# Sixteen modulation vectors of a two-layer fp32 mixer, summed on VectorE instead of multiplied on TensorE

## Chip, cores and metric

One core of a Trainium2 chip runs the whole program. The metric is the device time of one execution in microseconds (us); smaller is better. Engines are named as the profile names them: PE is TensorE's matmul, PEld its weight load, DVE is VectorE, ACT is ScalarE, POOL is GpSimd, SP is SyncE, which issues nearly all DMAs here.

## What is computed

Two layers over 512 latent tokens and 256 context tokens, width 1024, in fp32. Each layer makes shift, scale and gate vectors from two conditioning vectors (`c` and `c_ctx`), normalises the tokens with them, projects to twelve 512-wide sections and four 1024-wide gates, mixes the sections in four branches, and merges and projects them:

```python
mod_lat = jnp.dot(jax.nn.silu(c), w_mod) + b_mod          # [1024] x [1024, 3072]
mod_ctx = jnp.dot(jax.nn.silu(c_ctx), w_mod) + b_mod
sh_l, sc_l, g_l = jnp.split(mod_lat[:, None, :], 3, axis=-1)
z_lat = split_proj(jnp.dot(layer_norm(x) * (1.0 + sc_l) + sh_l, w_in) + b_in)
...                                                       # four branches: y_f, y_d, y_p, y_n
g = sigmoid(z[12].reshape(b, n, N_BRANCH, D_MODEL))
proj = einsum('bnie,ied->bnid', gated, w_branch)
out = einsum('bnd,de->bne', sum(g * proj, axis=2), w_out)
x_new = layer_norm(alpha * x + g_l * out_lat, ln_g, ln_b)
```

`w_mod` is 1024 x 3072 for each layer. The second layer takes no context output, so of its gate part only the latent vector is needed.

## The kernel before

Every fp32 product runs as three fp32r products of a high and a low part (`mm3`). Weights come in half tiles of 4 x 128 rows by 256 columns (512 KB) through one stream, `Stream`: `load` issues the DMA into a ring of three (`w_raw`), ACT casts the high part (`w_hi`, L333), DVE or POOL subtracts the low part (`w_lo`, L336), into rings of four. Jobs `take` their half tiles in the order of the list made by `jobs`; `ahead` splits the next ones during a job.

An order written out by hand sets everything else: `clk` counts modelled PE time, `chain` queues the steps behind a job with a delay each, and `turn_over`, called at each `yield` of a job, emits the steps that are due. Side work (attention, `side_na` and others) is a generator paced by the same clock. Each engine then runs its instructions in that order.

The stages of a layer: the first eight modulation columns (256 wide) of layer 0 ahead of everything; then the projections (`tok`, `rope`, `nat`), with the attention of the branches interleaved; the merges (`job_merge`, twelve jobs of a branch and a 256-wide column, each `gates`, `products`, `gates`, `products`), then `mgate` and `mproj` for the fourth branch; then `out`.

A modulation column is `job_mod`: it takes two half tiles, runs 16 matmuls with the conditioning vectors (4 columns: two vectors, high and low) as weights and 256 columns moving, ACT copies the 4 x 256 result (`rows`, L477), two small fp32 matmuls with `sel` turn it into columns (`turn`, L482), and DVE adds the bias (`add`, L488) into `modT`. Columns 8 to 11 of each layer stand between the halves of the `nat` sections 1, 5, 7 and 11, at the end of the projections; columns 0 to 7 of layer 1 stand behind the merges of branches 1 and 2 of layer 0.

PSUM tiles named `mm` are a ring of four banks (`mmt`). A merge part of layer 0 takes two of them (512 and 256 tokens), of layer 1 one.

Of the kernel before, what the change touches and what calls it, by code (L numbers as in the profile page):

```python
# [37 lines left out]
M_LAG = (0.4, 1.6, 2.0)  # L38
# [71 lines left out]
def emit(tc, A, out):  # L110
# [4 lines left out]
    def jobs():  # L115
        J = [("start",)] + [("mod", 0, c) for c in range(8)]
        for l in range(DEPTH):
# [59 lines left out]
    with ExitStack() as ctx, tc.manual_schedule():  # L177
# [4 lines left out]
        wr = pool("wr", 3)  # L182
        wp = pool("wp", 4)
# [169 lines left out]

        early = []
# [19 lines left out]
        cT = cp.tile([128, 8, 4], F32R, name="cT")  # L374

# [77 lines left out]
        def cond(ct):  # L453
            sg = vs.tile([16, 128], F32, name="csg", tag="vt")
            S.activation(sg, ct, AF.Sigmoid)
            V.tensor_tensor(out=ct, in0=ct, in1=sg, op=ALU.mult)
            ps = mmt()
            PE.transpose(ps[:, 0:16], ct, ident[:16, :16])
            pv = ps[:, 0:16].rearrange("p (v k) -> p k v", v=2)
            V.tensor_copy(cT[:, :, 0:2], pv)  # L460
            sub_lo(cT[:, :, 2:4], pv, cT[:, :, 0:2])

        def job_mod(l, c):
            hs = ws.take(2)
            ps = mmt()
            early_ = l == 0 and c < 8
            for k in range(8):
                for j in range(2):
                    mm(ps[0:4, 0:256], cT[:, k, :], hs[k // 4][j][:, k % 4, :], k == 0 and j == 0, k == 7 and j == 1)
                if k == (0 if early_ else 5):  # L470
# [20 lines left out]

            c2 = chain((M_LAG[0], rows), (M_LAG[1] if early_ else M_LAG[2], turn), (0.4, add), hold=[ps], reads=1, cls="mod", depth=1)

# [1231 lines left out]
        for j in J:  # L1725
# [39 lines left out]
            elif kind == "mod":  # L1765
# [5 lines left out]
                if l == 0 and j[2] < 8:  # L1771
                    for i in range(2, 6):
                        if X_AT[i - 2] == j[2]:
                            load_x(i)
                    norm_x(*X_NORM[j[2]])
# [23 lines left out]
            elif kind == "flag":  # L1799
                risen.append((j[1], [c for c in klass.get("tok", []) + klass.get("mt", []) if not c.done()]))  # L1800
# [29 lines left out]
            elif kind == "m_split":  # L1830
                finish_all()
                close_pool()
# [42 lines left out]
```

## Time and profile before

| | us |
|---|---|
| median of 3 runs (2042.03 to 2047.87) | 2044.71 |
| the profiled execution's own time | 2051.7 |
| its span | 2049.7 |
| PE busy | 1939.6 (95%) |
| DVE busy | 1145.4 (56%) |
| ACT busy | 899.5 (44%) |
| mean granted clock of TensorE, of full speed | 0.972 |

Busy time of PE is made of matmuls whose ends overlap, so the time that a group of matmuls takes is read from the starts of its first and of the next instruction in the timeline. The profiled execution is 2.0 us longer than its span, and 7.0 us over the median of the runs.

### The profile page before, as it was taken

What the parts mean: (1) busy time and instruction counts of PE and PEld (TensorE: products, weight loads), DVE (VectorE), ACT (ScalarE), POOL (GpSimd) and SP (SyncE); (2) the same over time, 40 slices, a digit from 0 to 9 for tenths busy, and PEclk for the clock granted to TensorE, in tenths of its full rate; (3) what the DMA queues carried; (4) which work ended last, traced back from release to release, by engine and by line L of the source; (5) the groups of instructions that cost most, each with busy time, mean ns of one, the idle gap of its engine ahead of it and who ended that gap; (6) DMA issues with size and microseconds to landing.
All of it is one profiled execution on the core that took longest, in us unless ns stands there. A gap on an engine that the chain in (4) does not pass through costs nothing.

```text
span 2049.7 us, 31044 instructions
## 1 busy us (share of the span) xinstructions
PE 1939.6 (95%) x11911; PEld 1679.0 (82%) x11911; DVE 1145.4 (56%) x2208; ACT 899.5 (44%) x1753; POOL 327.6 (16%) x322
## 2 busy tenths in 40 slices
PE   6999999988999999999999979998998999999996
PEld 3998888876888888888888979887877887888886
DVE  7636676554666432445316685577655775355368
ACT  5423465555566422323222254345554665333232
POOL 6321221201110000000000353122122210000013
PEclk9999999998999999999999979999999999999999
DMA  8423834335562531525212446364327655344344
GB/s 273 155 79 106 276 115 149 134 103 162 163 188 91 184 114 54 164 93 165 93 62 70 140 133 207 98 241 132 127 101 236 204 171 186 113 134 134 96 133 153
DMA packets 257396, 293.74 MB, mean 143 GB/s; under 512 B 25844, under 2 KB 220384, under 8 KB 256736
## 3 DMA queue, kind: packets, MB, share of 16 engines
q1 hardware_dynamic: 256672, 286.46, 43.6%
q0 software_dynamic: 576, 5.29, 0.7%
q8 instruction: 94, 1.54, 0.3%
q14 instruction: 54, 0.44, 0.1%
HBM read 230.82 MB, written 62.35 MB: 143 GB/s over the span
## 4 chain that ended last, share of the span: by engine, by line
PE 52%; DVE 7%; ACT 3%; DMA 2%; issue 2%; POOL 1%; SPq 0%; POOLq 0%; ACTq 0%; DVEq 0%
PE mm L268 46%; PE sd L268 4%; PE sd L272 1%; DMA w_raw<-in_w_out 1%; DVE w_lo L336 1%; DVE yt L1578 1%; DVE px0l L280 1%; DVE dp L955 1%; DMA w_raw<-in_w_in 0%; ACT w_hi L333 0%; ACT px0l L1046 0%; DVE dp L972 0%; PE mm L482 0%; DMA mtmp<-g 0%; DVE pws L797 0%
## 5 line engine op out<-in xcount | busy, mean ns | idle before, releaser
L336 POOL TENSOR_TENSOR w_lo<-w_raw,w_hi 128x512 fp32r<-128x512 f32 x148 | 208.3, 1418 | 1211.6 <-ACT w_hi L333 1136.8
L333 ACT CAST w_hi<-w_raw 128x512 fp32r<-128x512 f32 x520 | 300.0, 619 | 218.8 <-PE mm L268 113.9
L336 DVE TENSOR_TENSOR w_lo<-w_raw,w_hi 128x512 fp32r<-128x512 f32 x372 | 260.4, 732 | 202.9 <-ACT w_hi L333 201.4
L268 PE MATMUL mm<-px0h,w_hi 128*128 128x512 f32 x1216 | 339.2, 352 | 8.8 <-ACT w_hi L333 5.3
L268 PE MATMUL mm<-px0h,w_lo 128*128 128x512 f32 x1216 | 336.7, 350 | 0.6 <-DVE w_lo L336 0.6
L268 PE MATMUL mm<-px0l,w_hi 128*128 128x512 f32 x1216 | 334.1, 347 | 0.2 <-DVE px0l L1431 0.2
L268 PE MATMUL mm<-px1h,w_hi 128*128 128x512 f32 x864 | 290.8, 373 | 2.9 <-ACT sg L1471 2.3
L268 PE MATMUL mm<-px1h,w_lo 128*128 128x512 f32 x864 | 289.4, 371 | 0.0
L268 PE MATMUL mm<-px1l,w_hi 128*128 128x512 f32 x864 | 288.3, 370 | 0.0
L268 PEld LDWEIGHTS mm<-px0h,w_hi 128*128 128x128 f32 x1216 | 193.1, 191 | 39.8 <-ACT w_hi L333 6.3
L268 PEld LDWEIGHTS mm<-px0l,w_hi 128*128 128x128 f32 x1216 | 193.4, 191 | 31.3 <-issue 1.0
L268 PEld LDWEIGHTS mm<-px0h,w_lo 128*128 128x128 f32 x1216 | 192.3, 191 | 32.4 <-DVE w_lo L336 1.3
L268 PEld LDWEIGHTS mm<-px1h,w_hi 128*128 128x128 f32 x864 | 150.2, 189 | 32.0 <-ACT sg L1471 2.8
L268 PEld LDWEIGHTS mm<-px1h,w_lo 128*128 128x128 f32 x864 | 149.6, 189 | 28.3 <-issue 1.3
L268 PEld LDWEIGHTS mm<-px1l,w_hi 128*128 128x128 f32 x864 | 150.1, 189 | 27.6 <-issue 0.5
L268 PE MATMUL mm<-w_hi,px0h 128*128 128x256 f32 x480 | 144.5, 301 | 4.7 <-DVE px0h L552 4.3
L268 PE MATMUL mm<-w_lo,px0h 128*128 128x256 f32 x480 | 139.9, 292 | 6.7 <-POOL w_lo L336 6.0
L268 PE MATMUL mm<-w_hi,px0l 128*128 128x256 f32 x480 | 139.7, 291 | 0.7 <-DVE px0l L280 0.7
L268 PE MATMUL mm<-w_lo,px1h 128*128 128x256 f32 x384 | 112.4, 293 | 8.1 <-DVE w_lo L336 4.2
L268 PE MATMUL mm<-w_hi,px1h 128*128 128x256 f32 x384 | 114.3, 298 | 1.1 <-ACT w_hi L333 0.7
L268 PE MATMUL mm<-w_hi,px1l 128*128 128x256 f32 x384 | 111.5, 290 | 0.2 <-DVE px1l L280 0.2
L1503 DVE TENSOR_TENSOR mtmp<-mm,sg 128x512 f32<-128x512 f32 (+1 forms) x48 | 27.4, 599 | 142.9 <-PE mm L268 141.9
(234 smaller groups left out, 3110.3 us busy)
## 6 DMA issues: line engine op xcount, KB each, us to landing
w_raw<-in_w_in SPq DMA_DIRECT2D x160, 512.0 KB, 4.0
w_raw<-in_w_mod SPq DMA_DIRECT2D x36, 512.0 KB, 3.7
w_raw<-in_w_branch SPq DMA_DIRECT2D x32, 512.0 KB, 3.4
w_raw<-in_w_out SPq DMA_DIRECT2D x32, 512.0 KB, 3.5
w<-in_w_mod SPq DMA_DIRECT2D x12, 512.0 KB, 6.0
g<-ab SPq DMA_DIRECT2D x16, 384.0 KB, 2.7
nb<-bt SPq DMA_DIRECT2D x48, 128.0 KB, 4.7
y<-y SPq DMA_DIRECT2D x14, 384.0 KB, 4.9
```

The costliest lines, as they stand in the source:

```text
L268: PE.matmul(o, a, b, start=start, stop=stop)
L272: PE.transpose(o, i, idn)
L280: V.tensor_tensor(out=out_lo, in0=src, in1=hi.bitcast(F32), op=ALU.subtract)
L333: S.copy(x[1], x[0])
L336: e.tensor_tensor(out=x[2], in0=x[0], in1=x[1].bitcast(F32), op=ALU.subtract)
L955: V.tensor_scalar(out=p, in0=src, scalar1=-0.125, scalar2=None, op0=ALU.mult, op1=ALU.min, accum_out=mn)
L1503: V.tensor_tensor(out=o_[:, o:o + m], in0=ps[j][:, :m], in1=sg[:, o:o + m], op=ALU.mult)
L1578: V.scalar_tensor_tensor(out=y, in0=xs, scalar=ALPHA, in1=y, op0=ALU.mult, op1=ALU.add)
```

## The change

Sixteen of the 24 modulation columns leave `job_mod`: columns 8 to 11 of both layers and 0 to 7 of layer 1. They become jobs `vec`. Their weights no longer pass through `Stream`: they come by SP into a ring of two (`w_vec`) in fp32 and are not split. DVE multiplies each 128 x 256 slice by the conditioning vector's entry for its partition (`cS`, a copy of the conditioning vectors made at the start) and adds it up in `macc`: 8 steps for each vector and column, two vectors, or one where only the latent one is needed. The steps are spaced in modelled time (4 at 1.5, then 4 at 1.2). Then `total` sums over partitions with fp32 matmuls (`macc` as weights of 128 x 128, two columns of ones moving), and `add` puts the bias on. The twelve columns of layer 0's turn start behind the merges from the third of branch 0 to the last of branch 2, and behind the first two `mgate` jobs; the four of layer 1 behind its merges from the third of branch 0 on.

```diff
             for i, s in enumerate((1, 5, 7, 11)):
-                J += [("nat", l, s, 0), ("mod", l, 8 + i), ("nat", l, s, 1)]
-            mods = [("mod", l + 1, c) for c in range(8)] if l + 1 < DEPTH else []
+                J += [("nat", l, s, 0), ("nat", l, s, 1)]
+            mods = [("vec", l, 8 + i) for i in range(4)]
+            mods += [("vec", l + 1, c) for c in range(8)] if l + 1 < DEPTH else []
...
                         J += [("merge", l, b, s)]
-                        if b and mods:
+                        if mods and (b or s > 1):
                             J += [mods.pop(0)]
                 else:
-                    J += [("mgate", l, b, s) for s in range(4)] + [("mproj", l, b, s) for s in range(4)]
+                    for s in range(4):
+                        J += [("mgate", l, b, s)]
+                        if mods:
+                            J += [mods.pop(0)]
+                    J += [("mproj", l, b, s) for s in range(4)]
...
+        wm = pool("wm", 2)
...
+        class Vectors:
...
+            def load(self):
+                while self.nd < len(self.todo) and (self.nd < 2 or self.nd - 2 in self.ch and self.ch[self.nd - 2].done()):
+                    l, c, k = self.todo[self.nd]
+                    r = wm.tile([128, 4, 256], F32, name="w_vec", tag="w_vec")
+                    nc.sync.dma_start(r, half(w_mod[l], k, c * 256))
...
+                def weigh(k):
+                    r = self.raw[i + k // 4]
+                    for v in range(nv):
+                        a, x, w = acc[:, v, :], r[:, k % 4, :], cS[:, v, k:k + 1]
+                        if k == 0:
+                            V.tensor_scalar(out=a, in0=x, scalar1=w, scalar2=None, op0=ALU.mult)
+                        else:
+                            V.scalar_tensor_tensor(out=a, in0=x, scalar=w, in1=a, op0=ALU.mult, op1=ALU.add)
+                def total():
+                    st["p"] = mmt()
+                    for b in range(2):
+                        for v in range(nv):
+                            PE.matmul(st["p"][:, 4 * b + 2 * v:4 * b + 2 * v + 2], acc[:, v, b * 128:(b + 1) * 128], ones[:, 0:2].bitcast(F32),
+                                      start=True, stop=True)
...
+                self.load()
+                self.ch[i] = chain(*[(1.5, lambda k=k: weigh(k)) for k in range(4)])
+                ch = self.ch[i + 1] = chain((6.0, lambda: finish(self.ch[i])), (1.2, self.load), *[(1.2, lambda k=k: weigh(k)) for k in range(4, 8)],
+                                            (5.0, total), (0.6, add), cls="vec")
...
+            V.tensor_copy(cS, ps[:, 0:16].rearrange("p (v k) -> p v k", v=2))
...
+                if j[1] == "na":
+                    vec.load()
...
-    nc = bacc.Bacc("TRN2", target_bir_lowering=False, num_devices=1)
+    nc = bacc.Bacc("TRN2", target_bir_lowering=False, num_devices=1, dynamic_dma_scratch_size=4096)
```

The order on PE behind a merge of layer 0's second branch. Before, the last matmuls of the modulation column, then the next gates, whose tiles are `mm_8565` and `mm_8566`:

```order
L268 MATMUL mm_8520<-w_hi_8473,cT_108 4x256
L268 MATMUL mm_8520<-w_lo_8474,cT_108 4x256 [waits DVE_49]
L268 MATMUL mm_8520<-w_hi_8473,cT_108 4x256
L268 MATMUL mm_8520<-w_lo_8474,cT_108 4x256
L268 MATMUL mm_8565<-px0h_83,w_hi_8538 128x512 [waits Activation_49]
L268 MATMUL mm_8566<-px0h_83,w_hi_8538 128x256 [waits DVE_49]
```

Now the sum of a column stands inside the gates of a merge and nothing stands between two merges:

```order
L274 MATMUL mm_8323<-px0h_86,w_hi_8153 128x512
L274 MATMUL mm_8324<-px0h_86,w_hi_8153 128x256
L394 MATMUL mm_8374<-ones_95,macc_8207 128x2 [waits DVE_49] x2
L394 MATMUL mm_8374<-ones_95,macc_8207 128x2 x2
L274 MATMUL mm_8323<-px0l_87,w_hi_8153 128x512
L274 MATMUL mm_8324<-px0l_87,w_hi_8153 128x256
```

Sixteen matmuls and two small ones leave each such place, and four small ones with 128 weight columns come in, behind a wait for DVE.

The order on DVE in the same merges. Before (`y` and `px1l` prepare the next branch, `mtmp` and `mg` are a merge's products):

```order
L336 TENSOR_TENSOR w_lo<-w_raw,w_hi 128x512 [waits Activation_49]
L488 TENSOR_SCALAR modT_103<-mm,biasT_101 128x2 [waits PE_49]
L488 TENSOR_SCALAR modT_103<-mm,biasT_101 128x2
L1424 TENSOR_TENSOR y<-y,g 128x768 [waits DMAHW1_49,DMAHW0_49]
L336 TENSOR_TENSOR w_lo<-w_raw,w_hi 128x512 [waits DMAHW6_49,Activation_49]
L336 TENSOR_TENSOR w_lo<-w_raw,w_hi 128x512 [waits Activation_49]
L1431 SCALAR_TENSOR_TENSOR px1l<-y,px1h 128x768 [waits Activation_49]
```

Now:

```order
L1564 TENSOR_TENSOR mg_7378<-mg_7378,mtmp 128x768 [waits DVE_49]
L386 TENSOR_SCALAR macc<-w_vec,cS 128x256 [waits DMAHW0_49]
L386 TENSOR_SCALAR macc<-w_vec,cS 128x256
L388 SCALAR_TENSOR_TENSOR macc<-w_vec,cS,macc 128x256 [waits DVE_49] x2
L1482 TENSOR_TENSOR y<-y,g 128x768 [waits DMAHW5_49,DMAHW4_49]
L342 TENSOR_TENSOR w_lo<-w_raw,w_hi 128x512 [waits DMAHW1_49,Activation_49]
L388 SCALAR_TENSOR_TENSOR macc<-w_vec,cS,macc 128x256 [waits DVE_49] x2
L342 TENSOR_TENSOR w_lo<-w_raw,w_hi 128x512 [waits Activation_49]
L1489 SCALAR_TENSOR_TENSOR px1l<-y,px1h 128x768 [waits Activation_49]
L388 SCALAR_TENSOR_TENSOR macc<-w_vec,cS,macc 128x256 [waits DVE_49] x2
L388 SCALAR_TENSOR_TENSOR macc<-w_vec,cS,macc 128x256 [waits DMAHW2_49,DVE_49]
```

The weighing steps stand between the other work, in pairs, and the first of each half tile waits for its load.

The order on PE in layer 1's projections where its attention begins (`sd<-px0h` are scores, `np` probabilities). Before:

```order
L268 MATMUL sd_15703<-px0h_83 128x256 x12
L268 MATMUL mm_15688<-px1h_85,w_lo_15664 128x512
L268 MATMUL mm_15688<-px1h_85,w_hi_15663 128x512 [waits Activation_49]
L268 MATMUL mm_15688<-px1l_86,w_hi_15663 128x512
L268 MATMUL mm_15688<-px1h_85,w_lo_15664 128x512 [waits DVE_49]
L482 MATMUL mm_15734<-sel_98,mrow_15693 128x2 [waits Activation_49]
L482 MATMUL mm_15734<-sel_98,mrow_15693 128x2
L268 MATMUL mm_15688<-px1h_85,w_hi_15663 128x512
L268 MATMUL mm_15688<-px1l_86,w_hi_15663 128x512
L268 MATMUL mm_15688<-px1h_85,w_lo_15664 128x512
L268 MATMUL mm_15688<-px1h_85,w_hi_15671 128x512
L268 MATMUL mm_15688<-px1l_86,w_hi_15671 128x512
```

Now, from the same scores to the transposes of the probabilities:

```order
L274 MATMUL sd_15546<-px0h_86 128x256 x12
L274 MATMUL mm_15494<-px1l_89,w_hi_15482 128x512
L274 MATMUL mm_15494<-px1h_88,w_lo_15483 128x512 [waits DVE_49]
L274 MATMUL mm_15494<-px1h_88,w_hi_15482 128x512
L274 MATMUL mm_15494<-px1l_89,w_hi_15482 128x512
L274 MATMUL mm_15494<-px1h_88,w_lo_15483 128x512
L274 MATMUL mm_15494<-px1h_88,w_hi_15482 128x512 [waits Activation_49]
L274 MATMUL mm_15494<-px1l_89,w_hi_15482 128x512
L274 MATMUL mm_15494<-px1h_88,w_lo_15483 128x512 [waits DVE_49]
L274 MATMUL mm_15494<-px1h_88,w_hi_15482 128x512
L278 MATMUL sd_15593<-ident_90,np_15504 128x128 [waits DVE_49,PE_49]
L278 MATMUL sd_15593<-ident_90,np_15505 128x128 [waits DVE_49]
```

The turn of the modulation row (L482) with its wait for ACT is gone from there; nine matmuls stand between the scores and the transposes in both.

## Rows read from the trace of the kernel before

**Rows 1.** The page's first part: busy us, share of the span, instructions.

```profile
PE 1939.6 (95%) x11911; PEld 1679.0 (82%) x11911; DVE 1145.4 (56%) x2208; ACT 899.5 (44%) x1753; POOL 327.6 (16%) x322
```

**Rows 2.** Busy time by stretch: us, then PE PEld DVE ACT POOL (instructions), clock, DMA.

```profile
640.00:690.00 50.00, 49.95 (x335) 43.57 (x332) 25.41 (x59) 28.54 (x66) 0.00 (x0) 1.00 0.34 111
822.00:850.00 28.00, 28.00 (x166) 23.89 (x164) 15.70 (x25) 11.14 (x19) 0.00 (x0) 1.00 0.62 207
990.00:1018.00 28.00, 28.00 (x165) 23.92 (x166) 9.68 (x17) 7.97 (x15) 0.00 (x0) 1.00 0.31 95
1600.00:1700.00 100.00, 99.08 (x656) 81.68 (x655) 71.47 (x157) 67.36 (x144) 16.03 (x26) 1.00 0.57 175
```

**Rows 3.** Timeline of PE, one modulation column behind a merge: start us, us.

```profile
817.01 0.28 PE L268 MATMUL mm<-w_hi,cT 128*4 128x256 f32 x1
...
818.88 0.52 PE L268 MATMUL mm<-px0h,w_hi 128*128 128x512 f32 x2
...
821.65 0.51 PE L268 MATMUL mm<-px0h,w_lo 128*128 128x512 f32 x2
822.09 0.60 PE L482 MATMUL mm<-sel,mrow 4*128 4x2 f32 x4
822.62 0.62 PE L268 MATMUL mm<-px0h,w_hi 128*128 128x512 f32 x2
```

**Rows 4.** Groups of instructions, shapes apart: xcount | busy us, mean ns | idle before.

```profile
L268 PE MATMUL mm<-w_hi,cT 128*4 128x256 f32 x192 | 52.8, 304 | 3.5 <-ACT w_hi L333 3.5
L482 PE MATMUL mm<-sel,mrow 4*128 4x2 f32 x96 | 15.6, 264 | 5.9 <-ACT mrow L477 5.9
```

**Rows 5.** The same view, PE: an fp32 matmul with 128 x 128 weights.

```profile
L509 PE MATMUL sd<-gd,ones 128*128 128x512 f32 x12 | 7.4, 698 | 2.2 <-DVE gd L504 2.2
```

**Rows 6.** Timeline of PE: eight transposes in fp32 and what follows.

```profile
604.97 1.03 PE L272 MATMUL sd<-ident,np 128*128 128x128 f32 x8
605.76 0.59 PE L268 MATMUL mm<-px0h,w_hi 128*128 128x512 f32 x2
```

**Rows 7.** Groups, shapes apart: the DVE work that goes, and the nearest to what comes.

```profile
L336 DVE TENSOR_TENSOR w_lo<-w_raw,w_hi 128x512 fp32r<-128x512 f32 x372 | 260.4, 732 | 202.9 <-ACT w_hi L333 201.4 <-DMA y<-y 0.6
...
L972 DVE SCALAR_TENSOR_TENSOR dp<-dp,dr 128x256 f32<-128x256 f32 x8 | 3.9, 482 | 2.8 <-ACT dp L968 2.8
```

**Rows 8.** Tile `w_raw`, all its loads: from issue to landing.

```profile
DMA to landing us min/median/max: 3.3/3.9/13.2
```

**Rows 9.** Layer 1, a wait, ACT's timeline: start us, us, idle before in brackets.

```profile
1568.76 0.62 ACT L333 CAST w_hi<-w_raw 128x512 fp32r<-128x512 f32 x1 [7.47 <-DMA w_raw<-in_w_in]
...
1570.51 0.36 ACT L477 COPY mrow<-mm 4x256 f32<-4x256 f32 x1
```

**Rows 10.** The same wait, PE's timeline.

```profile
1564.62 0.40 PE L268 MATMUL mm<-px1h,w_lo 128*128 128x512 f32 x1
1570.92 1.01 PE L482 MATMUL mm<-sel,mrow 4*128 4x2 f32 x4 [5.91 <-ACT mrow L477]
```

**Rows 11.** The same place, DVE's timeline: the attention step that PE needs next.

```profile
1566.52 0.69 DVE L1259 CUSTOM_DVE_ANT_0 np<-sd,nb 128x512 f32<-128x512 f32 x1 [0.48 <-POOL nb L1224]
```

**Rows 12.** Busy time by stretch around that wait; columns as in rows 2.

```profile
1565.00:1571.00 6.00, 0.09 (x2) 0.08 (x1) 2.55 (x6) 2.24 (x6) 5.71 (x11) 0.71 1.02 318
1571.00:1576.00 5.00, 5.00 (x18) 4.39 (x19) 4.85 (x16) 3.13 (x8) 0.68 (x2) 0.50 1.06 353
```

**Rows 13.** Layer 0, PE timeline: the last attention matmuls of the projections.

```profile
673.58 0.88 PE L268 MATMUL sd<-px1l 128*128 128x256 f32 x6
```

**Rows 14.** Layer 1, chain that ended last: the projections' end.

```profile
1702.78 1.43 PE sd L268 x12
1704.21 7.97 PE mm L268 x35
```

More of the change, by code (lines that the diff above doesn't have):

```diff
@@ L37 @@
 SWAP = [(i + 16) % 32 for i in range(32)]
-M_LAG = (0.4, 1.6, 2.0)
+M_LAG = (0.4, 1.6)
 NORM_V = (0, 1, 2, 3, 4, 5)
@@ L352, in ahead, with __init__, run, add @@
                 self.split(self.cur + n - 1)
+        class Vectors:
+            def __init__(self):
+                self.todo = [(j[1], j[2], k) for j in J if j[0] == "vec" for k in (0, 4)]
+                self.nd, self.raw, self.ch = 0, {}, {}
+            def load(self):
[3 more added lines that the diff above has]
+                    nc.sync.dma_start(r, half(w_mod[l], k, c * 256))
+                    self.raw[self.nd] = r
+                    self.nd += 1
+            def run(self, l, c):
+                nv = 1 if c >= 8 and l + 1 == DEPTH else 2
+                acc, st = sm.tile([128, 2, 256], F32, name="macc", tag="macc", bufs=1), {}
+                i = self.todo.index((l, c, 0))
+                def weigh(k):
[12 more added lines that the diff above has]
+                                      start=True, stop=True)
+                    rings["mm"][1][slot[id(st["p"])][1]] = (ch, len(ch.st))
+                def add():
+                    for b in range(2):
+                        ct = 2 * c + b
+                        V.tensor_scalar(out=modT[l][:, ct, 0:nv], in0=st["p"][:, 4 * b:4 * b + 2 * nv:2],
+                                        scalar1=biasT[l][:, 93 + ct:94 + ct], scalar2=(1.0 if 8 <= ct < 16 else 0.0),
+                                        op0=ALU.add, op1=ALU.add)
+                self.load()
+                self.ch[i] = chain(*[(1.5, lambda k=k: weigh(k)) for k in range(4)])
+                ch = self.ch[i + 1] = chain((6.0, lambda: finish(self.ch[i])), (1.2, self.load), *[(1.2, lambda k=k: weigh(k)) for k in range(4, 8)],
+                                            (5.0, total), (0.6, add), cls="vec")
@@ L354, in emit @@
+        vec = Vectors()
         early = []
@@ L374, in emit @@
         cT = cp.tile([128, 8, 4], F32R, name="cT")
+        cS = cp.tile([128, 2, 8], F32, name="cS")
         def dt(name, shape):
@@ L465, in job_mod @@
             ps = mmt()
-            early_ = l == 0 and c < 8
             for k in range(8):
@@ L469, in job_mod @@
                     mm(ps[0:4, 0:256], cT[:, k, :], hs[k // 4][j][:, k % 4, :], k == 0 and j == 0, k == 7 and j == 1)
-                if k == (0 if early_ else 5):
+                if k == 0:
                     ws.ahead(2)
@@ L490, in add @@
                                     op0=ALU.add, op1=ALU.add)
-            c2 = chain((M_LAG[0], rows), (M_LAG[1] if early_ else M_LAG[2], turn), (0.4, add), hold=[ps], reads=1, cls="mod", depth=1)
+            c2 = chain((M_LAG[0], rows), (M_LAG[1], turn), (0.4, add), hold=[ps], reads=1, cls="mod", depth=1)
         def gate_rows(l, gb, tp):
@@ L1770, in emit @@
                 drive(job_mod(l, j[2]))
[L1771 to L1775, printed above, removed]
+                for i in range(2, 6):
+                    if X_AT[i - 2] == j[2]:
+                        load_x(i)
+                norm_x(*X_NORM[j[2]])
+            elif kind == "vec":
+                vec.run(l, j[2])
             elif kind == "tok2":
@@ L1831, in emit @@
                 finish_all()
+                vec.load()
                 close_pool()
```

## Prediction

> **What bounds the kernel now.** I began with the page's first part: PE is busy for 95% of the span, DVE for 56%, ACT for 44%, POOL for 16% [rows 1]. Such shares are averages, so I then read the stretches in which the moved work stands today, and those into which it goes [rows 2]. A merge of layer 0's middle branches takes 28.0 us and PE has no gap in it at the full clock, while DVE is busy for only 9.7 to 15.7 us. The ends of both projection stages, which hold the other columns, have PE at 49.95 of 50 and 99.1 of 100 us. So PE's time is what a change in these stages is worth, microsecond for microsecond, and DVE has room there. Third, the timeline of one column [rows 3]: what it takes of PE is read from starts, because the busy times of matmuls overlap. Last, the waits of PE: one of the sixteen columns stalls it for 5.91 us in layer 1 [rows 4, 10].
>
> **What goes from PE.** The 16 matmuls of a column take 818.88 - 817.01 = 1.87 us [rows 3]. The turn delays the gates: from the start of the last matmul pair ahead of it to the pair behind it is 822.62 - 821.65 = 0.97 us, where the pairs without it are 0.346 us apart (eight of them from 818.88 to 821.65), so it costs 0.62 us. Together 2.49 us for a column, and 16 columns make **39.8 us**. Layer 0's four and layer 1's four in the projections are interleaved with attention, but PE is as full there [rows 2], so I count them alike.
>
> **What comes to PE.** A column with two vectors brings four fp32 matmuls with 128 weight columns and two columns moving, one with one vector two. No row has just these. The nearest is the turn itself: it has 128 weight columns and two moving ones too, only 4 rows deep. Its two matmuls show as four records (96 records for 24 columns) [rows 4] and take 822.62 - 822.09 = 0.53 us [rows 3], that is 0.265 for one, and 0.09 to get in. Four then take 1.15 us, two 0.62. Twelve columns have two vectors and four have one (layer 1's gate part): 12 x 1.15 + 4 x 0.62 = **16.3 us**. The bounds: eight fp32 records of transposes take 605.76 - 604.97 = 0.79 us [rows 6], which gives 0.88 and 0.49 a column and 12.5 us; an fp32 matmul with 512 columns moving is 0.698 us a record [rows 5], so 8 of them 5.6 us, and the sum 12 x 5.6 + 4 x 2.8 = 78 us. I take the turn, which has the same weights' width and the same two moving columns; 512 moving columns are 256 times as many. On the weights' depth, the Trainium skill (TensorE: Matmul & The Clock Gate, LDWEIGHTS) says that loading takes the time of the columns, whatever the depth, about columns / 1.2 ns. An estimate by that is 0.107 us a record, 0.86 and 0.43 us a column and 12 us in all, 4 us better than by the turn's rows; the row, at 0.133 a record, decides for me until a run shows the 128-deep ones.
>
> PE's balance is 39.8 - 16.3 = **23.5 us gained**.
>
> **What goes to DVE, and what hides it.** A weighing step reads two SBUF tensors of 128 x 256; the like step of `dp` takes 0.482 us [rows 7]. There are 12 x 16 + 4 x 8 = 224 of them: 108 us. The `w_lo` of 16 columns, 64 at 0.732 us [rows 7], go: 47 us. DVE gains 61 us of work on balance, and all that is added lies in the merges. In a merge of layer 0 it takes up 16 x 0.482 = 7.7 us and loses 4 x 0.732 = 2.9: 14.5 to 20.5 of about 26.7 us. That is cover enough on the whole, so I cost it at nothing; if the cover goes, the price is that of the second rival. ACT loses 64 casts of 0.62 and 16 copies of 0.36 us [rows 9], 45 us; it is off the path, and that is worth nothing by itself.
>
> What is queued behind the new steps on DVE: `w_lo` of the next merge, which is wanted a merge part or more later; products, whose bank is wanted again after the next part; `px1l` of the next branch, two merges ahead. Each is late by one pair of steps, 1 us, at most, unless a step waits for its load.
>
> **The loads.** The same 512 KB per half tile come over the same queue, so the DMA's sum does not change. A half tile's second load is issued when the merge begins in layer 0, and DVE comes to it after the products of the last merge and four pairs of steps, some 6 us later; loads land after 3.9 us in the middle and 13.2 at worst [rows 8]. In layer 1, and behind the two `mgate` jobs, merges are shorter than a column's chain of steps: there the second load goes out only 1.2 us of modelled time before its first step. DVE then waits about 3 us, five times, with the next `w_lo` behind it. PE needs that one a part later, so I charge 0 to 3 us for three columns of layer 1, **1 us** in the sum. The SP queue's place for these loads is between two `w_raw` loads, and those wait for a `w_lo` that is already emitted; nothing new waits there.
>
> **The stall in layer 1.** The turn waits for ACT's copy, and ACT stands for 7.47 us at a cast whose load is late [rows 9]; PE idles from 1565.0 to 1570.9 [rows 10], and runs at 0.50 of its clock, the lower of the two levels, 1.2 GHz, for the next 5 us [rows 12], which is 2.5 us of work lost. All in all 8.4 us. In the new order the turn is not there, and the casts ahead of the probabilities belong to half tiles that were loaded earlier, since two of the column's own have gone from the stream. What is late next are the probabilities themselves: their last score step ends on DVE at 1567.2 [rows 11], and an exponential, a reciprocal and a scaling follow, so they are ready near 1569, while PE will have got there (five matmuls after 1564.9, 0.23 us each by the 35 of [rows 14]) at 1566. So 3 us of idling stay, and 8.4 - 3.2 = 5.2 would be gained with the clock up, 2.7 with it down for as long as before. I take **4 us**, with 0 and 8.4 as ends.
>
> The copy `cS` at the start lengthens a chain there by 0.2 us; a smaller scratch for POOL's DMAs touches four transfers, and I count nothing.
>
> **The sum** against the profiled execution: 2051.7 - 23.5 - 4 + 1 = 2025.2 us. It is 7.0 us over the median of the runs, so the forecast is **2018 us**, 1.3% faster.
>
> **Rivals.** *The gain in the projections is not had.* If the columns there only filled time in which attention was waiting anyway, their 8 x 2.49 = 19.9 us would come back as waits. Then 19.9 - 16.3 = 3.6 us are left, less 1 for the loads: 2044.7 - 2.6 = 2042 us, no change. For it speaks that attention's steps are chains over four engines; against it that PE hardly waits there [rows 2], and that after the last attention matmuls 16 us of projections are left in layer 0 (to 690) [rows 13] and 8 in layer 1 [rows 14], about as much as the 4 x 1.87 us of cover that go. Half of it lost would give 2028.
>
> *VectorE becomes the bound in the merges* (slower). The sum takes one of the four `mm` banks in the middle of a part, and a bank that it held is among the next part's; it comes free with DVE's `add`, about 2 us before that part begins. If DVE is later than that, PE waits, at the sum or at the next part. Were it late by half a column's weighing, 8 x 0.482 = 3.9 us, in each of the twelve columns of two vectors, that is 46 us: 2018 + 46 = 2064 us. It decides against the change from 27.5 / 12 = 2.2 us of lateness a column on. For it: DVE's work per merge grows by half, and its steps wait for loads. Against it: over 6 us of every merge remain free on DVE even in the fullest one.
>
> *The sums are dearer than the turn.* At the 0.698 us of rows 5 they would cost 78 instead of 16 us, and the time would be 2080. Only if moving two columns cost what 512 do; the turn speaks against it.
>
> *The change doesn't do what it says*, so that DVE's steps stay and PE's time too: the order shows that the matmuls are gone, so this has no chance of its own.
>
> **How the numbers follow.** Forecast 0.72 (its own range 2010 to 2026, from 0 to 8.4 us for the stall, 12.5 to 16.3 for the sums, 0 to 3 for the loads). Half of the projections' gain lost 0.09 (2028), all of it 0.08 (2042). VectorE as the bound 0.06 (2064), of which 0.01 with so little lateness that the time lies near 2045. Dear sums 0.01. A gain beyond the forecast, by short waits in the projections that go with the load on ACT and DVE, 0.04 (2005). The range of 2006 to 2036 leaves out the cases of 2042 and over and little more. A run of this kernel can tell 0.3%, 6.1 us, from no change: faster than 2038.6 holds the forecast, the half and the gain beyond it, 0.85; within 0.3% 0.09; slower 0.06.
>
> **What would show it.** Right: merges of layer 0 of about 25.5 us plus 1.15 us for the sum in place of 28.0, PE still without gaps; the records of the sum near 0.133 us apart; no wait of 5.9 us after layer 1's attention begins; DVE at about 1206 us busy, ACT at about 854. Wrong: waits of PE for `macc` or `modT` on DVE, or idle time of PE in layer 0's projections that was not there; a step of DVE waiting for `w_vec` by more than 4 us with PE waiting for the `w_lo` behind it.

## The result and the profile after

The changed kernel takes 2008.32 us in the median of four runs (2006.96 to 2013.54), the kernel before 2043.37 (2040.93 to 2047.87): a ratio of 0.983 with a 95% interval of 0.981 to 0.986, 35 us less. Run again with the experiments it took 2009.43 us against 2046.37, a ratio of 0.982 (0.981 to 0.984), 37 us less. The forecast was 2018 us, a gain of 27 us. Direction and range (2006 to 2036) held; the gain was 8 us larger than forecast, and the time lies 1.7 us below the forecast's own range of 2010 to 2026.

The page's first part of the changed kernel, beside [rows 1]:

```profile
PE 1901.0 (95%) x11703; PEld 1653.8 (82%) x11703; DVE 1185.4 (59%) x2369; ACT 861.7 (43%) x1673; POOL 329.9 (16%) x322
```

PE lost 38.6 us of busy time and stays at 95%; it is still the bound. DVE gained 40 us, ACT lost 38.

A merge of layer 0 and two of layer 1, busy time by stretch (columns as in [rows 2]; there a merge with a modulation column took 28.0 us):

```profile
805.70:832.00 26.30, 26.30 (x154) 22.92 (x153) 19.14 (x37) 7.73 (x13) 0.00 (x0) 1.00 0.47 157
1742.70:1759.60 16.90, 16.90 (x78) 14.05 (x78) 9.94 (x21) 5.37 (x10) 0.00 (x0) 1.00 0.60 193
1759.60:1777.10 17.50, 16.93 (x77) 13.81 (x76) 12.08 (x25) 5.59 (x10) 0.00 (x0) 1.00 0.67 213
```

PE has no gap in a merge of layer 0, and DVE has 7 us free. The sum itself, PE's timeline, beside [rows 3]:

```profile
763.96 0.51 PE L274 MATMUL mm<-px0h,w_hi 128*128 128x512 f32 x2
764.31 0.95 PE L394 MATMUL mm<-ones,macc 128*128 128x2 f32 x8
765.12 0.59 PE L274 MATMUL mm<-px0l,w_hi 128*128 128x512 f32 x2
765.55 0.51 PE L274 MATMUL mm<-px0h,w_lo 128*128 128x512 f32 x2
```

The eight records take 765.12 - 764.31 = 0.81 us, and the pair behind them 0.43 in place of 0.35: 0.89 us in all. From the second record on the starts are 0.112 us apart. The weighing steps and the sum, groups of instructions with shapes apart:

```profile
L388 DVE SCALAR_TENSOR_TENSOR macc<-w_vec,cS,macc 128x256 f32<-128x256 f32 x196 | 83.8, 478 | 3.5 <-DMA w_vec<-in_w_mod 3.3
L394 PE MATMUL mm<-ones,macc 128*128 128x2 f32 x112 | 13.5, 240 | 0.6 <-DVE macc L388 0.6
```

and the loads of the tile `w_vec`:

```profile
DMA to landing us min/median/max: 3.5/3.6/6.0
```

DVE waited for a load once, 3.3 us, in layer 1, and PE for a weighing step 0.6 us. Last, PE's waits in front of attention's scores (`sd<-px1h`) and probabilities (`np`) in layer 0, then in layer 1, where the wait of [rows 10] stood:

```profile
484.05 1.55 PE L274 MATMUL sd<-px1h 64*128 64x256 f32 x12 [2.90 <-DMA px1h<-nq]
...
494.63 0.45 PE L278 MATMUL sd<-ident,np 128*128 128x128 f32 x1 [4.00 <-DVE np L1329]
496.50 1.75 PE L278 MATMUL sd<-ident,np 128*128 128x128 f32 x7 [1.42 <-DVE np L1329]
...
1536.81 0.30 PE L278 MATMUL sd<-ident,np 128*128 128x128 f32 x1 [2.50 <-DVE np L1329]
1537.70 0.98 PE L278 MATMUL sd<-ident,np 128*128 128x128 f32 x7 [0.59 <-DVE np L1329]
```

The kernel before (its second execution, before_again) comes to the same scores of layer 0 without a wait, and waits less for the probabilities:

```profile
489.44 0.98 PE L268 MATMUL sd<-px1h 64*128 64x256 f32 x12
...
497.23 0.45 PE L272 MATMUL sd<-ident,np 128*128 128x128 f32 x1 [2.73 <-DVE np L1271]
498.84 1.76 PE L272 MATMUL sd<-ident,np 128*128 128x128 f32 x7 [1.17 <-DVE np L1271]
```

So in layer 0 waits of 2.9 and some 1.5 us came with the change.

To see where the time went I cut each profiled execution at the same marks, read from its timeline: layer 0's first projection matmul, in each layer the first sigmoid of the merges (`sg`), the first of the fourth branch (`sgs`) and the first product of `out` (`yt`), and the last `yt` product of layer 0, with which layer 1's projections begin. Lengths in us; the names are those of the experiments below:

| kernel | projections L0 | merges L0 | fourth branch L0 | projections L1 | merges L1 |
|---|---|---|---|---|---|
| before | 577.9 | 317.5 | 105.6 | 500.6 | 202.0 |
| before_again | 575.3 | 318.1 | 105.6 | 498.8 | 201.4 |
| changed | 556.4 | 303.9 | 107.5 | 484.7 | 204.4 |
| after_again | 558.9 | 305.9 | 105.9 | 483.7 | 204.9 |
| proj_only | 558.7 | 319.5 | 102.2 | 485.1 | 203.5 |
| merges_only | 576.1 | 305.0 | 104.8 | 500.2 | 202.1 |
| sum_twice | 556.6 | 313.2 | 109.0 | 484.4 | 208.3 |
| weigh_twice | 557.9 | 307.8 | 108.2 | 484.1 | 210.9 |
| ring_five | 576.7 | 318.8 | 103.9 | 496.7 | 201.9 |
| ahead_first | 577.5 | 319.6 | 103.9 | 504.7 | 201.7 |
| lead_back | 559.6 | 305.5 | 107.8 | 483.4 | 206.1 |
| casts_back | 560.1 | 306.1 | 107.2 | 484.2 | 204.3 |
| matmuls_back | 562.9 | 306.9 | 107.3 | 492.0 | 206.0 |
| gate_direct | 564.6 | 306.1 | 100.8 | 483.4 | 208.6 |

Layer 0's projections take 575 to 578 us with columns there (mean of before, before_again, merges_only and ring_five 576.5) and 556 to 559 without (mean of changed, after_again, proj_only, sum_twice and weigh_twice 557.7). That is 18.8 us for four columns, where the forecast had 4 x 2.49 = 10.0. This is the largest part of what it missed. The lengths are of one execution each: the spans of before and before_again are 42 us longer in the mean than those of changed and after_again, where the medians differ by 35 and 37, so some us of these differences belong to the executions and not to the kernels.

### The profile page after: what moved, and what is told of

The parts are those of the page before. It is cut to its first block, busy times and chain, and to the rows that moved or that the text cites. A ratio compares the mean times of both kernels' runs of the same rounds, so it can differ in the third digit from the quotient of the medians.

```text
span 2005.2 us, 30691 instructions
## 1 busy us (share of the span) xinstructions
PE 1901.0 (95%) x11703; PEld 1653.8 (82%) x11703; DVE 1185.4 (59%) x2369; ACT 861.7 (43%) x1673; POOL 329.9 (16%) x322
## 4 chain that ended last, share of the span: by engine, by line
PE 52%; DVE 7%; DMA 2%; ACT 2%; issue 2%; POOL 1%; SPq 1%; POOLq 0%; ACTq 0%; DVEq 0%
PE mm L274 46%; PE sd L274 4%; PE sd L278 1%; DVE yt L1636 1%; DVE w_lo L342 1%; DMA w_raw<-in_w_out 1%; PE mm L394 1%; DVE px0l L286 1%; DVE dp L1013 1%; DMA mtmp<-y 1%; ACT px0l L1104 0%; DMA px0h<-nv1h 0%; DVE dp L1030 0%; DVE yt L1633 0%; DMA w_vec<-in_w_mod 0%
## 5 line engine op out<-in xcount | busy, mean ns | idle before, releaser
L339 ACT CAST w_hi<-w_raw 128x512 fp32r<-128x512 f32 x456 | 263.6, 618 | 184.5 <-PE mm L274 120.3
L342 DVE TENSOR_TENSOR w_lo<-w_raw,w_hi 128x512 fp32r<-128x512 f32 x308 | 220.1, 735 | 152.0 <-ACT w_hi L339 149.9
L1529 ACT ACTIVATE sg<-mm,biasT 128x512 f32<-128x512 f32 x72 | 41.8, 615 | 153.8 <-PE mm L274 123.3
```

The costliest lines, as they stand in the source:

```text
L339: S.copy(x[1], x[0])
L342: e.tensor_tensor(out=x[2], in0=x[0], in1=x[1].bitcast(F32), op=ALU.subtract)
L1529: S.activation(sg[:, o:o + m], ps[j][:, :m], AF.Sigmoid, bias=biasT[l][:, ct:ct + 1])
```

## Experiments

**Which half brings what.** Two kernels take over half of the change each. `proj_only`:

```diff
             mods = [("vec", l, 8 + i) for i in range(4)]
-            mods += [("vec", l + 1, c) for c in range(8)] if l + 1 < DEPTH else []
+            heads = [("mod", l + 1, c) for c in range(8)] if l + 1 < DEPTH else []
...
+                        if b and heads:
+                            J += [heads.pop(0)]
```

> Columns 8 to 11 of both layers become vec jobs at the same places as in the changed kernel; columns 0 to 7 of layer 1 stay TensorE columns behind the merges of branches 1 and 2 of layer 0, as before. Forecast's steps: 8 x 2.49 = 19.9 us go, sums of 4 x 1.15 + 4 x 0.62 = 7.1 come, 4 for layer 1's stall, against a before near 2043: 2026 us. Second theory (the stalls in both layers' projections were part of the price of a column there, and the sums cost 0.86 and 0.43 us as read from the changed kernel's trace): 19.9 - 5.2 + 4 + some 6 of idle time and half clock in layer 0: 2018 us; the waits of PE for w_hi near 475 us of the span and for the mrow row near 1571 are gone. Rival (attention was waiting anyway, projections' gain not had): 2043 + 5 = 2048 us.

`merges_only`:

```diff
-                J += [("nat", l, s, 0), ("nat", l, s, 1)]
+                J += [("nat", l, s, 0), ("mod", l, 8 + i), ("nat", l, s, 1)]
-            mods = [("vec", l, 8 + i) for i in range(4)]
-            mods += [("vec", l + 1, c) for c in range(8)] if l + 1 < DEPTH else []
+            mods = [("vec", l + 1, c) for c in range(8)] if l + 1 < DEPTH else []
```

> Only columns 0 to 7 of layer 1 become vec jobs, behind the merges of branches 1 and 2 where the TensorE columns stood; columns 8 to 11 of both layers stay in the projections as before. Forecast's steps: 8 x 2.49 - 8 x 1.15 = 10.7 us less than before: 2032 us. Second theory (sum 0.86 us): 8 x 1.63 = 13.0 us less, 2030 us, with the waits of PE for w_hi near 475 us and for mrow near 1571 us still there. Rival (projections' gain not had): nearly all of the changed kernel's gain, 2010 us.

Against a before of 2048.07 us, proj_only took 2021.96 (ratio 0.987, 0.985 to 0.988) and merges_only 2035.19 (0.993, 0.992 to 0.995): 26 and 13 us, 39 together for the 37 of the whole. The rival that the projections' gain is not had falls; their eight columns bring twice as much as the eight behind the merges. Both results lie nearer to the second theory (25 and 13) than to the forecast's steps (17 and 11). In merges_only, where whole columns stand in the projections again, PE waits at layer 0's first column there, as in the kernel before; in proj_only it does not:

```profile
473.71 1.01 PE L273 MATMUL mm<-px0h,w_hi 128*128 128x512 f32 x2 [4.06 <-ACT w_hi L338]
```

**The price of a sum.** `sum_twice` issues each sum's matmuls twice:

```diff
-                    for b in range(2):
+                    for b in (0, 1, 0, 1):
                         for v in range(nv):
                             PE.matmul(st["p"][:, 4 * b + 2 * v:4 * b + 2 * v + 2], ...
```

> The changed kernel with each sum over partitions issued twice, into the same columns. By the turn's rows (0.265 us a matmul) 12 x 1.06 + 4 x 0.53 = 14.8 us more than the changed kernel: 2023 us. By the records of the sum in the changed kernel's trace (0.112 us apart, two a matmul): 12 x 0.90 + 4 x 0.45 = 12.6 us more: 2021 us. If moving two columns cost what 512 do: 70 us more. The spacing of layer 0's merges, 26.33 us now, tells the first two apart: 27.39 or 27.23.

It took 2022.36 us, 12.9 more than the changed kernel's 2009.43, or 11 when each is set against the before that was run beside it (2048.07 and 2046.37). PE's timeline of one doubled sum:

```profile
818.77 1.84 PE L394 MATMUL mm<-ones,macc 128*128 128x2 f32 x16
820.47 0.60 PE L274 MATMUL mm<-px0l,w_hi 128*128 128x512 f32 x2
```

1.70 us for 16 records, 0.89 more than for 8, so 0.11 us for each record that was added. Undisturbed merges of layer 0 stand 27.2 to 27.3 us apart in place of 26.3. The 0.133 us that the forecast took from the turn were 0.02 us a record too dear, and 512-wide rows have nothing to do with it. The turn's own records do not cost more: its four (4 weight rows) start 0.133, 0.111 and 0.112 us apart, and the rest of its time is the 0.176 us from the last of them to the gates.

**How much DVE can be late.** `weigh_twice` does every multiply-and-add step twice, the first time into a scratch tile:

```diff
                         else:
+                            V.scalar_tensor_tensor(out=idle_, in0=x, scalar=w, in1=a, op0=ALU.mult, op1=ALU.add)
                             V.scalar_tensor_tensor(out=a, in0=x, scalar=w, in1=a, op0=ALU.mult, op1=ALU.add)
```

> The changed kernel with each of the 196 multiply-and-add steps done twice, the first time into a scratch tile: 196 x 0.40 to 0.48 = 78 to 94 us more work on DVE, 5.6 to 6.7 us in a column with two vectors. If DVE's free time in a merge covers it (19.1 of 26.3 us busy in the fullest middle merge of the changed kernel), the time stays within 4 us of the changed kernel: 2008 to 2012 us. Rival (VectorE becomes the bound as soon as its steps are late): PE waits for macc 3.9 us or more in each of twelve columns: 2055 us or more.

2017.76 us, 8.3 more than the changed kernel (6.6 when each is set against its own before), with DVE's busy time up by 95 us to 1280.5. Two merges of layer 0 by stretch:

```profile
807.50:835.40 27.90, 26.74 (x154) 23.01 (x153) 25.82 (x51) 7.74 (x14) 0.00 (x0) 1.00 0.45 152
835.40:861.70 26.30, 26.30 (x154) 22.93 (x153) 22.26 (x49) 5.45 (x11) 0.00 (x0) 1.00 0.32 100
```

and from the answer for the tile `macc`, what its steps waited for and who waited for it (us, times):

```profile
  DMA w_vec<-in_w_mod: 5.2, 1
...
  PE mm L396: 5.2, 3
```

A merge with DVE at 22.3 of 26.3 us keeps its length; one with 25.8 us of DVE work is 1.6 us longer, 1.2 of it idle on PE. Of the loss, 6.2 us lie in layer 1's merges (210.9 in place of 204.7 us), where a step waits 5.2 us for a load, PE waits behind it, and then runs at half its clock:

```profile
1778.87 0.34 PE L396 MATMUL mm<-ones,macc 128*128 128x2 f32 x1 [4.14 <-DVE macc L390]
```

```profile
1778.80:1785.70 6.90, 6.83 (x19) 5.56 (x20) 6.26 (x14) 1.85 (x4) 0.00 (x0) 0.51 0.88 290
```

That is 3.5 us more of waiting than in the changed kernel (0.6) and 3.4 us of work lost to the clock. So the cover that I had counted as free is there in layer 0 and holds almost twice the weighing. In that merge of layer 1 DVE still has time, 14.9 of 21.0 us busy; what fails there is the load, which the step awaits for 5.2 in place of 3.3 us, and the steps behind it take twice as long. The rival's price, some 4 us in each of twelve columns, is not seen even so.

**Is it the same in another execution?** `after_again` and `before_again` are the two kernels unaltered.

> The changed kernel unaltered, on the chip of the other runs. The changed kernel's first runs were 0.983 of before's; against a before of 2048 that is 2013 us. If the shares add up (columns of the projections 2022 and columns behind the merges 2035, each against 2048), it is 2048 - 26 - 13 = 2009 us. Layer 0's projections take 556 to 559 us from first projection matmul to first gate, layer 1's from the last out block of layer 0 to the first gate 484 to 485, as in the other runs without columns there.

> The kernel before, unaltered, a second profile. If the waits of PE for w_hi near 475 us (4.06 us) and for mrow near 1571 us (5.91 us) belong to the program, both are there again, and layer 0's projections take 576 to 578 us, layer 1's 500. If they were a chance of one execution, they are gone or elsewhere.

2009.43 and 2047.70 us. The waits are there again in before_again. PE's and ACT's timeline at layer 0's first column in the projections:

```profile
469.18 0.28 PE L268 MATMUL mm<-w_lo,cT 128*4 128x256 f32 x1
473.46 1.01 PE L268 MATMUL mm<-px0h,w_hi 128*128 128x512 f32 x2 [4.00 <-ACT w_hi L333]
```

```profile
466.73 1.28 ACT L1113 ACT_TABLE_LOAD   x1
468.02 0.85 ACT L1113 ACTIVATE sq<-var 128x768 f32<-128x768 f32 x1
468.88 1.28 ACT L1114 ACT_TABLE_LOAD   x1
470.18 0.84 ACT L1114 ACTIVATE sq<-sq 128x768 f32<-128x768 f32 x1
470.93 1.03 ACT L754 ACTIVATE ab<-mm,biasT 128x512 f32<-128x512 f32 x2
471.85 1.05 ACT L759 ACTIVATE gz<-mm,biasT 128x512 f32<-128x512 f32 x2
472.78 2.19 ACT L333 CAST w_hi<-w_raw 128x512 fp32r<-128x512 f32 x4
```

and the stretch behind the wait, in before_again:

```profile
473.40:480.20 6.80, 6.14 (x18) 4.75 (x18) 4.89 (x7) 1.80 (x5) 0.00 (x0) 0.52 0.64 193
```

PE is through the column at 469.4 and needs the casts of the next half tile. ACT is busy without a gap from 466.7 on with an attention step (two table loads, two activations) and the last section's `ab` and `gz`; the casts stand behind them. PE waits 4.0 us, and then runs at the lower of its two clock levels, 1.2 GHz (0.52 of the clock granted), for 6.8 us. In the changed kernel this wait is not there (5.2 us of waits for `w_hi` in the whole execution, 10.0 in before_again).

**What makes that stall.** Two edits to the kernel before and three to the changed kernel. `ring_five` gives the weight loads two more buffers:

```diff
-        wr = pool("wr", 3)
+        wr = pool("wr", 5)
...
-                return i - (9 if i < 18 else 3)
+                return i - (9 if i < 18 else 5)
```

> The kernel before with five w_raw buffers in place of three, so that loads are issued two half tiles earlier (and the smaller scratch of the changed kernel, to make room). Theory: layer 1's stall of 5.91 us is a late load, so it goes: layer 1's projections 494 to 497 in place of 500 us; layer 0's wait of 4.06 us near 475 us is casts standing behind other work on ACT, so it stays, and layer 0's projections stay at 577: 2043 us against 2048. Rival: both are late loads; then layer 0's projections fall to 570 too: 2036 us. Rival: both are queueing on ACT; then no change, 2048 us.

2043.45 us, ratio 0.998 (0.997 to 1.000), 3 us less. Layer 1's wait for the row is down from 5.2 and 5.9 to 2.3 us (PE's timeline) and its projections to 496.7 us; layer 0's stay at 576.7. As the theory had it: layer 1's stall was mostly a late load, layer 0's was not.

```profile
1566.20 1.00 PE L482 MATMUL mm<-sel,mrow 4*128 4x2 f32 x4 [2.29 <-ACT mrow L477]
```

`ahead_first` calls for the casts earlier in a column:

```diff
-                if k == (0 if early_ else 5):
+                if k == 0:
```

> The kernel before with one number changed: a column's call for the next two half tiles' casts comes at its first step in place of its sixth. On ACT three of the four casts then stand ahead of the two activations of the nat section instead of behind them. Theory (layer 0's stall is ACT's queue): the wait of 4.06 us near 475 us shrinks by the 1.9 us that the two activations take, the wait of 1.25 us near 541 us goes, and layer 0's projections take 572 to 574 us in place of 577; layer 1's stall (a late load) stays: 2044 us against 2048. Rival (late loads in both): no change.

2050.84 us, 1.002 (1.001 to 1.003): 4.5 us more. PE's and ACT's timeline at the same place:

```profile
472.90 0.50 PE L268 MATMUL mm<-px0h,w_hi 128*128 128x512 f32 x1 [2.13 <-ACT w_hi L333]
475.46 0.58 PE L268 MATMUL mm<-px0h,w_hi 128*128 128x256 f32 x1 [2.06 <-ACT gz L759]
```

```profile
472.24 1.64 ACT L333 CAST w_hi<-w_raw 128x512 fp32r<-128x512 f32 x3
473.79 1.04 ACT L754 ACTIVATE ab<-mm,biasT 128x512 f32<-128x512 f32 x2
474.73 1.04 ACT L759 ACTIVATE gz<-mm,biasT 128x512 f32<-128x512 f32 x2
```

The wait shrank by the 1.9 us that I had said, but the layer's projections did not (577.5 us). The 256-wide matmul that follows writes a bank that `gz` has yet to read, and `gz` now stands behind the casts: 2.13 + 2.06 is as long as before. Behind a column of 1.87 us PE needs two things of ACT at once, the next casts and the last part's bank, and both stand behind the attention step. The wait near 541 us stays as well, 1.21 us, now for `gz`. In layer 1 the same edit made the stall 9.8 us and the projections 504.7, which is the run's whole loss; why it grew there stays open. My expectation for this run was wrong.

`lead_back`, `casts_back` and `matmuls_back` put one side of a column back into the changed kernel each, at its eight places in the projections:

```diff
+            late = sec in SEC_G and s == 0
...
-                                 after=((3, lambda: ws.ahead(1)) if f == 0 else (5, lambda: ws.ahead(2))))
+                                 after=((9 if late else 3, lambda: ws.ahead(1)) if f == 0 else (6 if late else 5, lambda: ws.ahead(2))))
```

> The changed kernel, but at the eight places in the projections where a modulation column stood, the casts of the next two half tiles are called for at the end of the nat half ahead (1.0 us of PE time before they are wanted in layer 0, 0.7 in layer 1), as late as behind a column. No matmul and no cast is added. Theory (the rest of the gain in layer 0's projections, 18.8 - 10.0 = 8.8 us, is the late call for casts behind ACT's other work): the wait of PE for w_hi near 475 us is back with some 4 us, layer 0's projections take 563 to 567 in place of 557.7 us, layer 1's 488 to 490 in place of 484.4: 2018 to 2022 us against 2009. Rival (it is ACT's work, the casts themselves): within 3 us of 2009.

```diff
+            def cast():
+                if sec in SEC_G and s == 0:
+                    for _ in range(2):
+                        idle_ = sm.tile([128, 2, 256], F32, name="macc", tag="macc", bufs=1)
+                        S.copy(idle_.rearrange("p v (h n) -> p (v h) n", h=2).bitcast(F32R), ident[:, None, :].to_broadcast([128, 4, 128]))
...
-                                 after=((3, lambda: ws.ahead(1)) if f == 0 else (5, lambda: ws.ahead(2))))
+                                 after=((3, lambda: (cast(), ws.ahead(1))) if f == 0 else (5, lambda: (cast(), ws.ahead(2)))))
```

> The changed kernel with four casts of 128x512 on ACT put back at each of the eight places (out of a constant, into a tile that nobody reads there), ahead of the casts of the next half tiles; the call for these stays as early as in the changed kernel. 32 x 0.57 us = 18 us more work on ACT. Theory (late call): within 3 us of the changed kernel's 2009 us, layer 0's projections at 558 to 560. Rival (ACT's work): layer 0's projections 562 to 566, 2014 to 2018 us.

```diff
-                J += [("nat", l, s, 0), ("nat", l, s, 1)]
+                J += [("nat", l, s, 0), ("idle", l), ("nat", l, s, 1)]
...
+        def job_idle(X):
+            ps = mmt()
+            for k in range(8):
+                for j in range(2):
+                    mm(ps[0:4, 0:256], cT[:, k, :], X.h[:, k, 256 * j:256 * j + 256], k == 0 and j == 0, k == 7 and j == 1)
+                yield
```

> The changed kernel with 16 matmuls of a modulation column's shape put back at each of the eight places, fed from the tokens that are in SBUF; no load, no cast, no turn, and their result is read by nobody. Theory (PE's time counts in full in the projections): 8 x 1.87 = 15 us more, 7.5 in each layer: layer 0's projections 565, layer 1's 492, 2024 us against 2009. Rival (a matmul there fills time in which attention is waiting anyway): half or less, 2009 to 2016 us.

Against a before of 2046.60 us: lead_back 2012.72 (0.983, 0.981 to 0.985), casts_back 2010.09 (0.982, 0.980 to 0.983), matmuls_back 2023.57 (0.989, 0.987 to 0.991). The matmuls cost 14 us of the 15 that they take, so PE's time counts nearly in full in the projections; in the profiled execution 7.6 us of it lie in layer 1 and 5.2 in layer 0. The late call alone and the casts alone bring 3 and 1 us, within the intervals; neither brings the wait for `w_hi` back. In lead_back three of the four casts stand ahead of ACT's table loads, because without the column the call comes earlier in the order:

```profile
463.85 1.66 ACT L339 CAST w_hi<-w_raw 128x512 fp32r<-128x512 f32 x3
465.52 1.28 ACT L1172 ACT_TABLE_LOAD   x1
```

So my theory of the late call fell in that form. What the runs show is that the stall belongs to the column as a whole: it is there in each kernel that has unaltered columns in layer 0's projections (4.00 to 4.06 us in before, before_again, merges_only and ring_five) and in none without them, and no single side of a column brings it back. That it takes the column's short PE time, the call within it and ACT's busy stretch together is argued from the rows of before_again and ahead_first, not shown. The column's matmuls with the late call, and no casts of its own, were not run together; that combination stays open.

**A further step, tried.** The gate's sums can be made with ones as weights and the weighed columns moving, which gives each partition the whole row and drops the six spreads in `out`. `gate_direct`:

```diff
+                    if c >= 8:
+                        for v in range(nv):
+                            PE.matmul(st["p"][:, v * 256:(v + 1) * 256], ones.bitcast(F32), acc[:, v, :], start=True, stop=True)
...
+                            g = gk[l][v][:, (c - 8) * 256:(c - 7) * 256]
+                            V.tensor_tensor(out=g, in0=st["p"][:, v * 256:(v + 1) * 256], in1=g, op=ALU.add)
...
-            rows = list(gate_rows(l, gb, ep)) if (g, qs) == (0, (0,)) else []
+            rows = []
...
+                gp = open_pool(f"gk{l}")
+                gk[l] = [gp.tile([128, D], F32, name=f"gb{v}") for v in range(2 if l == 0 else 1)]
+                for g in gk[l]:
+                    nc.sync.dma_start(g, A["b_mod"][l:l + 1, 2 * D:3 * D].broadcast_to([128, D]))
                 mp = open_pool(f"mp{l}")
...
-    nc = bacc.Bacc(..., dynamic_dma_scratch_size=4096)
+    nc = bacc.Bacc(..., dynamic_dma_scratch_size=2048)
```

> The changed kernel, but the sums of columns 8 to 11 are made with ones as weights and the 256 sums of a vector moving, so that each partition gets the gate's row at once; the bias is there ahead of it by a load, and the six spreads of the gate rows (an fp32 matmul of 512 columns from a diagonal each) leave the start of the out stage. PE loses 6 x 0.98 us and two waits of 1.1 us for the diagonals, and 4 x 0.86 + 4 x 0.45 us of sums; it gets 12 times two fp32 records of 256 columns, some 0.5 us each: 8.0 + 5.2 - 6.0 = 7 us less, 2002 us against 2009. Rival (out's first matmuls wait for the last product anyway): 4 us less, 2005 us.

2013.00 us (0.983, 0.981 to 0.985): nothing gained on the changed kernel. In its own place the step did more than expected: the fourth branch of layer 0 up to `out` takes 100.8 us in place of 105.9 to 107.5, and that of layer 1 65.0 in place of 69.8. It was given back elsewhere, most of it at the start of the merges, which the table counts with layer 0's projections (564.6 us). PE's, then ACT's timeline:

```profile
692.81 1.01 PE L274 MATMUL mm<-px1h,w_hi 128*128 128x512 f32 x2 [6.54 <-ACT sg L1538]
```

```profile
686.39 0.84 ACT L1494 ACTIVATE px1h<-y 128x768 fp32r<-128x768 f32 x1 [13.10 <-DMA mtmp<-y]
```

I had issued the bias rows' broadcast loads, two of 512 KB, just ahead of the loads that prepare the merges' input; these landed late, ACT began `px1h` at 686.4 us in place of 679.5, and PE waited 6.5 us where the changed kernel waits 1.4. That the broadcast loads made them late is read from their order and was not tested. Layer 1's merges lost 4 us more. With these loads issued later the step might pay; that was not run.

## Why the prediction was right, and where it was short

- **What bounds the kernel** held: microsecond for microsecond on PE. proj_only, merges_only and matmuls_back each show it.
- **What goes from PE**, 2.49 us a column, was 0.11 us short. The reading stopped at the start of the pair behind the turn, and that pair is slower too, 0.46 us (822.62 to 823.08) in place of 0.35. With 2.60 us a column, eight columns less nine sums of 0.89 make 12.8 us; layer 0's merges became 12.9 us shorter (means of two executions each). The line behind the last one of [rows 3] that this is read from:

```profile
823.08 0.40 PE L268 MATMUL mm<-px0l,w_hi 128*128 128x512 f32 x1
```

- **What comes to PE** was the first mis-sized term: 16.3 us forecast, 0.133 us a record; a sum costs 0.89 us, 0.112 a record, with half of that for one vector, so 12.5 us in all. The failed step was to divide the turn's time by its four records, with the way out among them, and to multiply by eight: inside the turn, too, the records are 0.112 us apart, so the depth of the weights made no difference. The transposes, which I had as a bound, give the 12.5 us. By the Trainium skill (TensorE: Matmul & The Clock Gate, LDWEIGHTS), by columns / 1.2 ns, the estimate was 0.107 us a record. The spacing in the trace agrees with it to 0.005 us, and it is the same for 4 and for 128 weight rows.
- **The projections** were the second, and the larger. "Layer 0's four and layer 1's four in the projections are interleaved with attention, but PE is as full there [rows 2], so I count them alike" rests on two stretches, 640 to 690 and 1600 to 1700 us. The columns at 470 and 540 us lie in neither; PE waits 4.0 us for casts behind the first and 1.25 behind the second. All in all layer 0's projections gained 18.8 us, not 10.0: PE's idle time there is 4.2 us less (30.3 to 26.1, means of the same four and five executions, length less busy time) and the time lost to the lower clock 3.7 us less (15.0 to 11.3, length times one less the mean granted clock). 0.9 us of the 18.8 is left, of which the 0.11 us a column above is 0.4; single executions differ by up to 5 us in the clock's part. The idle time is a balance: about 8 us of waits went, and the 2.9 and 1.5 us for `px1h` and `np` came, so the first rival, attention waiting in the columns' place, was true in a small part.
- **The stall in layer 1**: forecast 4 us, with "3 us of idling stay". Layer 1's projections gained 15.5 us (means of before and before_again, changed and after_again), so 5.5 beside the matmuls. The wait that I named as next, for the probabilities `np`, is there with 2.50 + 0.59 us: the mechanism was right, the size 1.5 us short. Part of that is that [rows 12] stopped too early: the lower clock lasted 1.7 us longer, so that 3.4 and not 2.5 us of work were lost behind the wait in that execution. The stretch behind that of [rows 12]:

```profile
1576.00:1577.70 1.70, 1.70 (x6) 1.19 (x4) 1.70 (x3) 0.59 (x1) 1.64 (x3) 0.50 0.11 34
```

- **DVE and the loads**: no price for the cover, which held in layer 0, and 1 us for late loads. DVE waits for a load once in place of five times, 3.3 us as estimated, and PE 0.6 us behind it; layer 1's merges grew by 3.0 us (four sums of 0.45 and 1 us of waits), forecast 3.5. DVE's busy time rose by 40, not 61 us; one reason is that steps issued back to back overlap, so that 196 of them are busy for 83.8 us and not for 196 x 0.48 = 94. The rest of that difference I did not break down.
- The rivals: VectorE as the bound is refuted by weigh_twice, dear sums by sum_twice, projections without gain by proj_only. The last, "A gain beyond the forecast, by short waits in the projections that go with the load on ACT and DVE", at 0.04 and 2005 us, is the one that came nearest to what happened, and I had given it too little: I had looked for such a stall in layer 1 alone. All the misses above have the same sign, so none hid another; the stated range held by 2.3 us because it reached down almost to that rival.
- Not forecast: `out` and the end of layer 1 took 60.2 us in place of 58.4 (two executions each), where the other kernels range from 57.2 to 63.0; these runs can't tell it from chance. Of the signs of being wrong, two came in small: PE's 0.6 us for `macc`, and the new waits in layer 0's projections.

## What to carry to other kernels

Before a group of matmuls is priced by its own length, look at what PE waits for just behind it, at every place where it stands and not at one: a short job between two long ones leaves the engines that feed the long ones only its own length as cover. Work moved off a full PE pays in full as long as the engine that takes it has the time, and its loads come in time, in the shortest stage that takes it up: here layer 0's merges had room for nearly twice the weighing, while in layer 1's a load was already 3.3 us late. And price a small matmul by the spacing of records inside a group, with the way in and out counted once; a doubled copy on the chip settles it.

## What the runs showed of the hardware

An fp32 matmul with 128 x 128 weights and two columns moving costs 0.22 us (two records, 0.112 us each), half of what a 256-wide one with ones as weights costs: PE's timeline of gate_direct gives 0.68 us for four such records and 0.19 more for the pair behind them.

```profile
773.18 1.02 PE L394 MATMUL mm<-macc,ones 128*128 128x256 f32 x4
773.86 0.70 PE L274 MATMUL mm<-px0l,w_hi 128*128 128x512 f32 x2
774.40 0.52 PE L274 MATMUL mm<-px0h,w_lo 128*128 128x512 f32 x2
```

A wait of PE in a full stretch costs more than its length: behind the 4.0 us of before_again stood 6.8 us at 0.52 of the clock, 3.3 us of work. And whether a shorter wait is followed by such a stretch changes from one execution of a kernel to the next: in layer 0's projections the changed kernel lost 8.5 us to the clock in one execution and 13.7 in the other.
